# RWKV-7 in a two-layer trunk: the inverse applied inside the scan, with part of its work moved from TensorE to VectorE and from VectorE to GpSimd

## The chip, the cores and the metric

The kernel runs on one core of a Trainium2 chip, which has five engines with an instruction list of their own: TensorE (PE, matrix products into PSUM), VectorE (DVE), ScalarE (ACT), GpSimd (POOL) and SyncE (SP, which issues most of the DMA transfers). Each engine works through its list in order; semaphores make one wait for another. The metric is the device time of one execution in microseconds (us).

## What is computed

Two layers over 512 tokens of width 1024, in float32. Layer 0 has a Griffin recurrent block and RWKV-7 beside each other, layer 1 a gated DeltaNet and an mLSTM; each layer is followed by a squared-ReLU MLP. The change is in RWKV-7 (8 heads of 64), whose core is this, cut from the reference:

```
def step(S, inp):
    rt, wt, kt, vt, kkt, at = inp
    sk = jnp.einsum('bhvk,bhk->bhv', S, kkt)
    S = (S * wt[:, :, None, :] - sk[..., None] * (kkt * at)[:, :, None, :]
         + vt[..., None] * kt[:, :, None, :])
    return S, jnp.einsum('bhvk,bhk->bhv', S, rt)
...
y = jnp.concatenate([ya, yb], axis=-1) @ ev_w_out[e]
```

`ya` is the Griffin block's result, `yb` RWKV's after a norm over each head and a gate.

## The kernel before

The kernel takes RWKV's recurrence in 8 chunks of 64 tokens. Within a chunk the tokens' corrections depend on each other through a lower triangular 64x64 matrix for each head; the kernel inverts one plus that matrix, and with the inverse a chunk is a handful of 64x64 products, with the state `S` (64x64 for each head) handed from chunk to chunk. A product for all 8 heads of one chunk is 8 matmuls of 64x64. Most tiles hold two chunks; the inverse is made for two **halves** of four chunks each (`hf` 0 and 1, earlier and later tokens).

The class `Net` writes each engine's list at build time. The steps are generators ("streams"); a planner keeps a modelled clock for each engine and resumes the stream whose operands are ready, so the code's order isn't the list's order. All instructions go through one helper, so the profile gives them all line 73 and one goes by the tiles' names. These streams matter:

- The projections of the normed input (`ps_g<-hT,wh` and `ps_g<-hT,wl`: the weights' high and low parts, which VectorE, ScalarE and GpSimd make from `raw`, straight from memory). They come in the order of k, r, v, x (Griffin's input) and z (Griffin's gate).
- `product_stream` (from line 877) multiplies `va` (scaled kk and r) with `kb` (scaled k and kk·a), `ps_a<-va,kb` 64x128, and masks the results into `ab` (the matrix to be inverted), `bk` and `mm` (within a chunk). Before, its last quarter waits for the first half's inverse (`xb0`).
- `inverse_stream` (from 955), once for each half: it writes `ab` to memory (`d<-ab`) and reads it back as `q` so that each partition holds one 32x32 block. `lanes` (from 930) inverts the blocks by forward substitution, 31 steps of two operations (`xtmp<-xt,q`, then `xt<-xt,xtmp`), with between 16 and 136 elements in a partition. The result goes to memory (`d<-xt`) and comes back as `xb` with the blocks in their places (`xb<-d`, 8 transfers). To join two 32x32 blocks into a 64x64 inverse, TensorE transposes the blocks (`ps_a<-idn,xb`, 32 matmuls a half, copied to `xs`), multiplies them by `ab` (`xs,ab`, copied to `xg`) and by `xb` (`xb,xg`), and VectorE adds.
- `turn_stream` (from 902) transposes four tensors to token order (`ps_a<-idn,va` and `ps_a<-idn,kb`, copied to `tm`). Ahead of that `kb` is scaled by `pc` on GpSimd (`kb<-kb,pc`).
- `ahead_stream` (1014 to 1043) makes, for two chunks at a time, `wt` (`xb,tm`), `bv` (`tm,ab`) and `u0` (`bv,xb`).
- `scan_stream` (1045 to 1101) goes through the chunks: `u = u0 + wt·S` (`S,wt`, added by VectorE into `us`), the next state from `tm,tm` and `us,tm` (added to `tt`, the decayed state, which GpSimd makes from `S`), and the output from `tm,mm`, `S,va` and `us,mm`.
- `lru_stream` is the Griffin block: VectorE makes `xc` (the convolution) in three steps from PSUM, TensorE its gates (`xc,wlru`), GpSimd `i` and `r`, VectorE the scans (`th<-xc,i`), GpSimd `gel`, and VectorE the high and low parts `yah` and `yal`.
- `out_k` (709) is the Griffin half of the output projection (`wh,yah`, `wl,yah`, `wh,yal`; 96 matmuls in two column halves), which fills TensorE between the scan's steps; `out_y` is RWKV's half. `load_x` reads the residual `x` again.

Of the kernel before, what the change touches and what calls it, by code (L numbers as in the profile page):

```python
# [83 lines left out]
class Net:  # L84
# [792 lines left out]
    def product_stream(self):  # L877

        nc = self.nc
        self.ab, self.bk, self.mu, self.mv = [None] * 2, [None] * 2, [None] * 4, [None] * 4  # L880
# [3 lines left out]
        for m, hf in ((1, 0), (1, 1), (0, 0), (0, 1)):  # L884
            if m == 0 and hf:
                yield "xb0"
            ab, mm = (self.bk, self.mv) if m == 0 else (self.ab, self.mu)
            ab[hf] = self.slot(shape=(P, 4, 4, 64), tag="q", name="ab")
            for j in (2 * hf, 2 * hf + 1):
                mm[j] = self.slot(shape=(P, 2, 4, 64), name="mm")  # L890
            for c in range(4 * hf, 4 * hf + 4):
# [4 lines left out]
                for k, (o, mask) in enumerate(((ab[hf][:, c % 4], self.lt64), (mm[c // 2][:, c % 2], self.le64))):  # L896
# [5 lines left out]
    def turn_stream(self):  # L902

        nc = self.nc
        self.tm = [[None] * 4 for _ in range(4)]
        for p in range(4):
            yield f"v{p}"
        for hf in range(2):
            yield f"cm0{hf}"
            cs = slice(4 * hf, 4 * hf + 4)  # L910
# [4 lines left out]
            for k, src in ((1, self.va[:, 1]), (0, self.va[:, 0]), (2, self.kb[:, 0]), (3, self.kb[:, 1])):  # L915
# [14 lines left out]
    def lanes(self, d1, at):  # L930
# [25 lines left out]
    def inverse_stream(self, hf):  # L956
# [10 lines left out]
        lanes = self.lanes(d1.rearrange("g l s t -> (g l) s t"), at)  # L967
# [14 lines left out]
        for i in range(2):  # L982
            ps = yield from self.take()
            for l in range(8):
                for r in rows:
# [3 lines left out]
            self.give(ps)  # L989
# [1088 lines left out]
```

## Time and profile before

| | us |
|---|---|
| median of 3 runs (1371.24 to 1372.73) | 1372.07 |
| the profiled execution's own time | 1372.95 |
| its span in the trace | 1371.2 |

| engine | busy, us | share of the span |
|---|---|---|
| TensorE | 1309.5 | 95% |
| VectorE | 773.1 | 56% |
| ScalarE | 476.1 | 35% |
| GpSimd | 193.3 | 14% |

The busy share is an average over stages with different limits. A row of the timeline gives the start, the duration, the engine, the operation with its result and operands, the shape and the number of instructions merged, and in brackets the idle time of the engine before it and what released it. TensorE does each float32 matmul of 64x64 in two passes, so the trace has two records for one matmul of the list. TensorE's granted clock is 1.0 at full speed (2.4 GHz) and 0.5 at the lower level (1.2 GHz).

### The profile page before, as it was taken

The page shows a single profiled execution, that of the slowest core. Times are in us where ns is not written, and L with a number is a line of the kernel's source. Part 1 is how long each engine was busy: PE and PEld are TensorE (multiplying, and loading weights), DVE is VectorE, ACT ScalarE, POOL GpSimd, SP SyncE. Part 2 cuts the span into 40 slices and gives each one's busy share as a digit, 9 for nine tenths or more (in the row PEclk, how much of TensorE's full clock was granted, in tenths as well). Part 3 has the DMA queues.
Part 4 walks back from the last instruction along what each step waited for, and adds up shares of the span by engine and source line. Part 5 has one row for each costly group of instructions (what it writes and reads, how often), then busy time and mean ns, then how long its engine had stood idle before and what let it go on. Part 6 is the DMA issues. An engine that isn't in the chain of part 4 may idle for free.

```text
span 1371.2 us, 20609 instructions
## 1 busy us (share of the span) xinstructions
PE 1309.5 (95%) x8372; PEld 1078.5 (79%) x8372; DVE 773.1 (56%) x1435; ACT 476.1 (35%) x823; POOL 193.3 (14%) x172
## 2 busy tenths in 40 slices
PE   5899878999999999999999989999899999999998
PEld 5678668978888888888896777888688888888886
DVE  4896795466534445344567747854754354453544
ACT  5633452324322323223453434421343232232223
POOL 2362232131000000000013512212500000000000
PEclk9999998999999999999999999999999999999999
DMA  6123123032222222222312222110422222222221
GB/s 233 62 77 97 48 60 100 4 120 88 75 95 92 93 94 104 95 92 92 108 55 85 77 85 78 49 52 9 138 77 86 99 92 93 92 94 98 101 93 62
DMA packets 58453, 118.11 MB, mean 86 GB/s; under 512 B 17270, under 2 KB 17526, under 8 KB 58358
## 3 DMA queue, kind: packets, MB, share of 16 engines
q1 hardware_dynamic: 57062, 114.68, 24.8%
q10 hardware_dynamic: 1296, 2.11, 0.5%
q8 instruction: 66, 1.08, 0.3%
q14 instruction: 29, 0.24, 0.1%
HBM read 113.10 MB, written 3.67 MB: 85 GB/s over the span
## 4 chain that ended last, share of the span: by engine, by line
PE 81%; DVE 10%; ACT 3%; issue 2%; DMA 2%; POOL 1%; SPq 0%; DVEq 0%; POOLq 0%; ACTq 0%
PE ps_a L73 61%; PE ps_g L73 20%; DVE wl L73 1%; DMA q<-d1g 1%; DVE xn L73 1%; DVE xtmp L73 1%; DVE xt L73 1%; DVE th L73 1%; DVE sft L73 1%; DVE x L73 1%; DVE ktok L73 0%; DMA gb<-in_g_norm_dram 0%; POOL w L73 0%; ACT junk L73 0%; DVE cv L73 0%
## 5 line engine op out<-in xcount | busy, mean ns | idle before, releaser
L73 DVE TENSOR_TENSOR wl<-raw,wh 128x512 fp32r<-128x512 f32 x329 | 234.1, 717 | 255.9 <-ACT wh L73 246.4
L73 PE MATMUL ps_a<-hT,wh 128*128 128x512 f32 (+1 forms) x1088 | 312.5, 372 | 0.0
L73 ACT CAST wh<-raw 128x512 fp32r<-128x512 f32 x285 | 173.7, 619 | 367.7 <-PE ps_a L73 311.8
L73 PEld LDWEIGHTS ps_a<-hT,wh 128*128 128x128 f32 x1088 | 197.7, 188 | 36.5
L73 PE MATMUL ps_g<-hT,wh 128*128 128x512 f32 x656 | 217.5, 410 | 8.2 <-DVE xt L73 4.1
L73 PE MATMUL ps_a<-hT,wl 128*128 128x512 f32 (+1 forms) x544 | 202.9, 373 | 0.0
L73 PEld LDWEIGHTS ps_g<-hT,wh 128*128 128x128 f32 x656 | 125.4, 193 | 42.1 <-issue 13.6
L73 PE MATMUL ps_a<-wh,acth 128*128 128x512 f32 x384 | 151.6, 395 | 0.0
L73 PE MATMUL ps_a<-wh,actl 128*128 128x512 f32 x384 | 151.5, 394 | 0.0
L73 PE MATMUL ps_a<-wl,acth 128*128 128x512 f32 x384 | 151.4, 394 | 0.0
L73 PE MATMUL ps_g<-hT,wl 128*128 128x512 f32 x328 | 130.6, 398 | 0.0
L73 POOL TENSOR_TENSOR wl<-raw,wh 128x512 fp32r<-128x512 f32 x39 | 52.2, 1349 | 553.9 <-ACT wh L73 553.9
L73 PEld LDWEIGHTS ps_a<-hT,wl 128*128 128x128 f32 x544 | 102.3, 188 | 19.3
L73 PEld LDWEIGHTS ps_a<-wh,actl 128*128 128x128 f32 x384 | 72.2, 188 | 17.1
L73 DVE CAST wh<-raw 128x512 fp32r<-128x512 f32 x83 | 37.7, 454 | 84.9 <-PE ps_a L73 83.4
L73 PEld LDWEIGHTS ps_a<-wl,acth 128*128 128x128 f32 x384 | 72.1, 188 | 17.0
L73 PEld LDWEIGHTS ps_a<-wh,acth 128*128 128x128 f32 x384 | 72.1, 188 | 16.7
L73 ACT ACTIVATE relu<-ps_a 128x512 f32<-128x512 f32 x60 | 35.9, 599 | 138.7 <-PE ps_a L73 138.7
L73 PEld LDWEIGHTS ps_g<-hT,wl 128*128 128x128 f32 x328 | 63.1, 192 | 15.0 <-issue 1.4
L73 PE MATMUL ps_g<-hT,w 128*128 128x256 f32 x384 | 51.5, 291 | 0.5 <-DVE hT L73 0.5
L73 PE MATMUL ps_g<-wl,acth 128*128 128x512 f32 x128 | 50.5, 395 | 0.0
L73 PE MATMUL ps_g<-wh,actl 128*128 128x512 f32 x128 | 50.5, 394 | 0.0
(405 smaller groups left out, 1833.2 us busy)
## 6 DMA issues: line engine op xcount, KB each, us to landing
raw<-in_w_up_dram SPq DMA_DIRECT2D x64, 512.0 KB, 3.2
raw<-in_w_down_dram SPq DMA_DIRECT2D x64, 512.0 KB, 3.2
raw<-in_w_in_dram SPq DMA_DIRECT2D x47, 512.0 KB, 3.3
raw<-in_w_out_dram SPq DMA_DIRECT2D x32, 256.0 KB, 2.8
x<-in_x_dram SPq DMA_DIRECT2D x4, 512.0 KB, 9.3
x<-in_x_dram SPq DMA_DIRECT2D x8, 256.0 KB, 4.9
gb<-in_g_norm_dram ACTq DMA_DIRECT2D x8, 256.0 KB, 3.5
raw<-in_w_in1t_dram SPq DMA_DIRECT2D x8, 256.0 KB, 2.8
```

Of the source, the lines that this page charges most:

```text
L73: return fn(*args, **kw)
```

## The change

- The inverse is applied inside the scan. `ahead_stream` and its products are gone. For each chunk TensorE makes `bk·v`, adds `alpha·S` (`S,va`) in the same PSUM tile, the sum is copied to `us`, multiplied by `xb` (`us,xb`), and copied again as `u`. The transposes of alpha (half of `idn,va`) are gone with `wt`.
- Of the first products (`product_stream`) the last quarter no longer waits for the first half's inverse.
- The transposes of 32x32 blocks ahead of the join are 4 VectorE operations (128x512) instead of 64 matmuls and 4 copies.
- The substitution of the second half (`hf` 1) is on GpSimd, that of the first half and of layer 1 stays on VectorE.
- `turn_stream` does its second half when the scan is through chunk 1. `x` is read again in two parts, the second after the first column half of `out_k`.

The core of the diff:

```diff
@@ product_stream
-            if m == 0 and hf:
-                yield "xb0"
@@ turn_stream
+            if hf:
+                yield "go0"
...
-            for k, src in ((1, self.va[:, 1]), (0, self.va[:, 0]), (2, self.kb[:, 0]), (3, self.kb[:, 1])):
+            for k, src in ((0, self.va[:, 0]), (1, self.kb[:, 0]), (2, self.kb[:, 1])):
@@ lanes
-            nc.vector.tensor_tensor(out=tmp[:, :m, :n], in0=xt[:, :m, j:j + 1].broadcast_to([P, m, n]),
+            eng.tensor_tensor(out=tmp[:, :m, :n], in0=xt[:, :m, j:j + 1].broadcast_to([P, m, n]),
...
-            nc.vector.tensor_tensor(out=xt[:, :m, j + 1:32], in0=xt[:, :m, j + 1:32], in1=tmp[:, :m, :n], op=ALU.subtract)
+            eng.tensor_tensor(out=xt[:, :m, j + 1:32], in0=xt[:, :m, j + 1:32], in1=tmp[:, :m, :n], op=ALU.subtract)
@@ inverse_stream
-        lanes = self.lanes(d1.rearrange("g l s t -> (g l) s t"), at)
+        lanes = self.lanes(d1.rearrange("g l s t -> (g l) s t"), at, (nc.vector, nc.gpsimd)[hf])
...
-                    nc.tensor.matmul(ps[r, l * 64:l * 64 + 64], lhsT=xb[r, 8 * i + l, :], rhs=self.ident[r, r], start=True, stop=True)
...
-            self.cpy(xs[i].rearrange("p l t -> p (l t)"), ps)
+            nc.vector.transpose(out=xs[i].rearrange("p l t -> p (l t)"), in_=xb[:, 8 * i:8 * i + 8].rearrange("p l t -> p (l t)"))
@@ scan_stream (new; ahead(c) makes bk·v into w, k·v into s and mv·v into the output)
+            if c:
+                yield self.need(S0)
+                product(quarters(w), self.va[:, 1, :, c], S0, False, True)
+            bv = us[:, 0]
+            self.cpy(bv, quarters(w))
...
+            if c:
+                product(yv, self.va[:, 2, :, c], S0, False, False)
...
+            product(quarters(ps), self.xb[c // 4][:, c % 4], bv, True, True)
+            u = us[:, 1]
+            self.cpy(u, quarters(ps))
...
+                product(quarters(s), self.tm[2][j][:, h], u, False, True)
...
+            product(yv, self.mu[j][:, h], u, False, h == 1)
...
+            if c < 7:
+                w, s = yield from ahead(c + 1)
```

Over the whole program TensorE's list goes from 6822 to 6630 matmuls, VectorE's from 1437 to 1387 instructions, GpSimd's from 177 to 230. The next rows are the lists themselves, with no time in them.

GpSimd, from the clearing of the second half's `xt` on. `ab`'s mask is followed before by the two scalings of `kb`:

```order
47 L73 MEMSET xt_1015 64x16
48 L73 TENSOR_TENSOR ab_857<-ab_857,cst 128x1024 [waits DMAHW5_49,DMAHW6_49,DMAHW4_49,DMAHW7_49,DVE_49,Pool_49]
49 L73 TENSOR_TENSOR ab_904<-ab_904,cst 128x1024 [waits DMAHW2_49,DMAHW1_49,DMAHW3_49,DMAHW0_49,DVE_49]
50 L73 TENSOR_TENSOR kb<-kb,pc_104 128x4x256 [waits PE_49]
51 L73 TENSOR_TENSOR kb<-kb,pc_104 128x4x256
```

And in the changed kernel, at the same place:

```order
47 L73 MEMSET xt_1064 64x16
48 L73 TENSOR_TENSOR ab_857<-ab_857,cst 128x1024 [waits DMAHW5_49,DMAHW6_49,DMAHW4_49,DMAHW7_49,DVE_49,Pool_49]
49 L73 TENSOR_TENSOR ab_904<-ab_904,cst 128x1024 [waits DMAHW2_49,DMAHW1_49,DMAHW3_49,DMAHW0_49,DVE_49]
50 L73 TENSOR_TENSOR xtmp_1065<-xt_1064,q_1063 128x31 [waits DMAHW7_49]
51 L73 TENSOR_TENSOR xt_1064<-xt_1064,xtmp_1065 128x31 [waits Pool_49]
52 L73 TENSOR_TENSOR kb<-kb,pc_104 128x4x256 [waits PE_49]
53 L73 TENSOR_TENSOR xtmp_1065<-xt_1064,q_1063 128x30 [waits Pool_49]
54 L73 TENSOR_TENSOR xt_1064<-xt_1064,xtmp_1065 128x30 [waits Pool_49]
```

The first step of the second half's substitution, with its wait for `q`, now stands ahead of the one scaling of `kb` left there; the other is on VectorE.

SyncE, where the two halves' `q` are read (`q_923` is the first half's). Before:

```order
34 L73 DMA d_1_1009<-ab_904 32x16x32 [waits DMAHW3_49]
35 L73 DMA raw_1048<-in_w_in_dram 128x1024 [waits DMAHW4_49,DVE_49,Pool_49]
36 L73 DMA q_923<-d_0_907 128x1x1024 [waits DMAHW7_49,DMAHW6_49,DMAHW5_49]
37 L73 DMA raw_1092<-in_w_in_dram 128x1024 [waits DVE_49]
38 L73 DMA raw_1134<-in_w_in_dram 128x1024 [waits DVE_49]
39 L73 DMA q_1014<-d_1_1009 128x1x1024 [waits DMAHW2_49,DMAHW3_49,DMAHW1_49,DMAHW0_49]
```

And after:

```order
34 L73 DMA d_1_1058<-ab_904 32x16x32 [waits DMAHW3_49]
35 L73 DMA q_923<-d_0_907 128x1x1024 [waits DMAHW6_49,DMAHW7_49,DMAHW5_49,DMAHW4_49]
36 L73 DMA raw_1099<-in_w_in_dram 128x1024 [waits DVE_49,Pool_49]
37 L73 DMA raw_1141<-in_w_in_dram 128x1024 [waits DVE_49]
38 L73 DMA q_1063<-d_1_1058 128x1x1024 [waits DMAHW2_49,DMAHW3_49,DMAHW1_49,DMAHW0_49]
```

The first `q` moves ahead of a weight load, and the second stands behind two loads instead of three.

TensorE, between the last projection (z's fourth) and the first matmuls of `out_k` (`wh,yah`). Before (`ab_857` and `xb_1732` are the first half's):

```order
651 L73 MATMUL ps_g_1780<-hT_108,wl_1699 128x512
652 L73 MATMUL ps_a_1885<-idn,xb_1732 64x64 [waits DMAHW4_49,DMAHW3_49,DMAHW5_49,DMAHW2_49,Pool_49]
653 L73 MATMUL ps_a_1885<-idn,xb_1732 64x64 [waits DMAHW6_49,DMAHW7_49,DMAHW1_49,DMAHW0_49]
654 L73 MATMUL ps_a_1885<-idn,xb_1732 64x64 x14
655 L73 MATMUL ps_a_1904<-idn,xb_1732 64x64 x16
656 L73 MATMUL ps_g_1923<-wh_1746,yah_1849 128x512 [waits DVE_49,Activation_49]
```

And after (`xs_1895`, `xs_1897`, `ab_904` and `xb_1755` are the second half's):

```order
661 L73 MATMUL ps_g_1843<-hT_108,wl_1774 128x512
662 L73 MATMUL ps_a_1899<-xs_1895,ab_904 64x64 [waits DVE_49,Activation_49]
663 L73 MATMUL ps_a_1899<-xs_1895,ab_904 64x64 x15
664 L73 MATMUL ps_a_1918<-xs_1897,ab_904 64x64 [waits DVE_49,Activation_49]
665 L73 MATMUL ps_a_1918<-xs_1897,ab_904 64x64 x15
666 L73 MATMUL ps_a_1952<-xb_1755,xg_1916 64x64 [waits DMAHW2_49,DMAHW1_49,DMAHW3_49,DVE_49,DMAHW4_49,Activation_49,Pool_49]
667 L73 MATMUL ps_a_1952<-xb_1755,xg_1916 64x64 [waits DMAHW6_49,DMAHW7_49,DMAHW5_49,DMAHW0_49]
668 L73 MATMUL ps_a_1952<-xb_1755,xg_1916 64x64 x14
669 L73 MATMUL ps_a_1970<-xb_1755,xg_1935 64x64 [waits Activation_49]
670 L73 MATMUL ps_a_1970<-xb_1755,xg_1935 64x64 x15
671 L73 MATMUL ps_g_2002<-wh_1821,yah_1938 128x512 [waits DVE_49]
```

Where the first half's transposes stood, the whole join of the second half now stands ahead of `out_k`; the first half's join follows among `out_k`'s first matmuls. On VectorE the transposes for `xs` stand behind the last of the Griffin scans and ahead of the cast `yah`.

## Rows read from the trace of the kernel before

**Rows 1.** The page, parts 1 and 4: busy time, and the chain by engine.

```profile
PE 1309.5 (95%) x8372; PEld 1078.5 (79%) x8372; DVE 773.1 (56%) x1435; ACT 476.1 (35%) x823; POOL 193.3 (14%) x172
...
PE 81%; DVE 10%; ACT 3%; issue 2%; DMA 2%; POOL 1%; SPq 0%; DVEq 0%; POOLq 0%; ACTq 0%
```

**Rows 2.** Windows: start and end, length, each engine's busy time, clock, DMA share, GB/s.

```profile
158.00:198.00 40.00, 39.56 (x157) 29.56 (x156) 38.49 (x88) 23.52 (x32) 14.55 (x12) 0.98 0.14 47
198.00:213.00 15.00, 5.09 (x67) 4.14 (x67) 14.37 (x28) 7.15 (x12) 8.34 (x5) 0.71 0.66 196
213.00:300.00 87.00, 86.63 (x1977) 78.30 (x1978) 46.57 (x91) 27.08 (x48) 17.51 (x16) 0.97 0.15 45
```

**Rows 3.** Timeline of TensorE from 202 to 212 us, then of VectorE at 209 us.

```profile
202.28 0.44 PE L73 MATMUL ps_a<-idn,xb 64*64 64x64 f32 x2 [4.72 <-DMA xb<-d]
204.88 3.32 PE L73 MATMUL ps_a<-idn,xb 64*64 64x64 f32 x62 [2.17 <-DMA xb<-d]
211.27 0.77 PE L73 MATMUL ps_g<-wh,yah 128*128 128x512 f32 x1 [3.06 <-DVE yah L73]
...
209.71 1.42 DVE L73 CAST yah<-gel 128x512 fp32r<-128x512 f32 x1
```

**Rows 4.** Timeline of TensorE from 155 to 158 us.

```profile
155.74 3.00 PE L73 MATMUL ps_a<-xc,wlru 128*128 128x512 f32 x4 [3.97 <-issue]
157.75 1.42 PE L73 MATMUL ps_g<-hT,wh 128*128 128x512 f32 x1
```

**Rows 5.** Timeline of TensorE from 222 to 226 us: products.

```profile
222.78 1.92 PE L73 MATMUL ps_a<-va,kb 64*64 64x128 f32 x32
224.53 1.10 PE L73 MATMUL ps_a<-xb,tm 64*64 64x64 f32 x32
225.46 1.10 PE L73 MATMUL ps_a<-tm,ab 64*64 64x64 f32 x32
```

**Rows 6.** Timeline from 229 to 240 us: the state's copy and addition.

```profile
232.55 0.37 ACT L73 COPY S<-ps_a 128x256 f32<-128x256 f32 x1 [0.76 <-PE ps_a L73]
...
236.35 0.42 DVE L73 TENSOR_TENSOR S<-ps_a,tt 128x256 f32<-128x256 f32 x1 [1.44 <-PE ps_a L73]
```

**Rows 7.** Timelines: SyncE's issues of `q` and `xb`, then VectorE where `q` lands.

```profile
116.72 0.66 SPq L73 DMA_DIRECT2D q<-d  x1
...
128.00 0.54 SPq L73 DMA_DIRECT2D q<-d  x1
...
197.98 5.24 SPq L73 DMA_DIRECT2D xb<-d  x8
...
131.68 0.19 DVE L73 TENSOR_TENSOR xtmp<-xt,q 128x31 f32<-128x31 f32 x1 [1.49 <-DMA q<-d]
...
144.74 0.19 DVE L73 TENSOR_TENSOR xtmp<-xt,q 128x31 f32<-128x31 f32 x1 [8.03 <-DMA q<-d]
```

**Rows 8.** Groups of GpSimd by form: count, busy us, mean ns, idle before.

```profile
L73 POOL TENSOR_TENSOR wl<-raw,wh 128x512 fp32r<-128x512 f32 x39 | 52.2, 1349 | 553.9 <-ACT wh L73 553.9
...
L73 POOL TENSOR_TENSOR kb<-kb,pc 128x1024 f32<-128x1024 f32 x4 | 8.0, 2014 | 0.0
...
L73 POOL TENSOR_TENSOR tt<-S,pc 128x256 f32<-128x256 f32 x6 | 3.7, 620 | 54.0 <-DVE S L73 33.3 <-ACT S L73 20.7
...
L73 POOL COPY vx<-ei 128x4 f32<-128x4 f32 x4 | 0.9, 237 | 0.0
```

**Rows 9.** DMA issues by line: KB each, median us from issue to landing.

```profile
d<-xt SPq DMA_DIRECT2D x2, 256.0 KB, 4.1
```

**Rows 10.** Tile `xt`, both layers: count, minimum/median/maximum ns, first and last start.

```profile
L73 DVE TENSOR_TENSOR xtmp<-xt,q x93: 183/260/1415, 131.7 to 883.8; 128x126 f32<-128x126 f32 x9, 128x30 f32<-128x30 f32 x6, 128x56 f32<-128x56 f32 x6, 128x78 f32<-128x78 f32 x6
L73 DVE TENSOR_TENSOR xt<-xt,xtmp x93: 180/261/1390, 132.0 to 884.0; 128x126 f32<-128x126 f32 x9, 128x30 f32<-128x30 f32 x6, 128x56 f32<-128x56 f32 x6, 128x78 f32<-128x78 f32 x6
```

**Rows 11.** Timelines of GpSimd and VectorE from 169 to 172 us.

```profile
169.69 2.07 POOL L73 TENSOR_TENSOR r<-xc 128x512 f32<-128x512 f32 x2
...
170.78 1.12 DVE L73 TENSOR_TENSOR xt<-xt,xtmp 128x126 f32<-128x126 f32 x1
```

More of the change, by code (lines that the diff above doesn't have):

```diff
@@ L712, in out_k @@
             yield from self.acc_steps(acc, ys)
+            if load is not None and ch == 0:
+                load(x, 1)
             for t in range(NT):
@@ L904, in turn_stream @@
         nc = self.nc
-        self.tm = [[None] * 4 for _ in range(4)]
+        self.tm = [[None] * 4 for _ in range(3)]
         for p in range(4):
@@ L1048, in scan_stream, with product, ahead @@
         S = self.slot(shape=(P, 2, 4, 64), name="S")
+        us = self.slot(shape=(P, 2, 4, 64), name="us")
         self.in_parts(S, 256)
-        us = self.slot(shape=(P, 2, 4, 64), name="us")
         self.in_parts(us, 256)
-        quarters = lambda ap: ap.rearrange("p (q x) -> p q x", x=64)
+        quarters = lambda ap: ap[:, 0:256].rearrange("p (q x) -> p q x", x=64)
+        vy = {}
+        def product(out, a, b, start, stop):
+            for q, r in self.HEADS:
+                nc.tensor.matmul(out[r, q], lhsT=a[r, q], rhs=b[r, q], start=start and q == 0, stop=stop and q == 3)
+        def ahead(c):
+            j, h = c // 2, c % 2
+            yield f"tm2{j // 2}"
+            if h == 0:
+                psy = yield from self.take()
+                vy[j] = psy, psy.rearrange("p (c q x) -> p c q x", c=2, q=4)
+            v = self.tm[0][j][:, h]
+            w = yield from self.take()
+            product(quarters(w), self.bk[j][:, h], v, True, c == 0)
+            yield
+            s = None
+            if c < 7:
+                s = yield from self.take()
+                product(quarters(s), self.tm[1][j][:, h], v, True, False)
+                yield
+            product(vy[j][1][:, h], self.mv[j][:, h], v, h == 0, False)
+            return w, s
+        yield "cm00"
+        w, s = yield from ahead(0)
         for c in range(8):
@@ L1089, in scan_stream @@
+            yield f"xb{c // 4}"
+            yield self.need(bv, self.xb[c // 4])
+            ps = yield from self.take()
+            product(quarters(ps), self.xb[c // 4][:, c % 4], bv, True, True)
+            u = us[:, 1]
+            self.cpy(u, quarters(ps))
+            self.give(ps)
             yield self.need(u)
             if c < 7:
-                for q, r in self.HEADS:
-                    nc.tensor.matmul(v[r, q], lhsT=bt[r, h, q, :], rhs=u[r, q, :], start=False, stop=(q == 3))
+                product(quarters(s), self.tm[2][j][:, h], u, False, True)
@@ L1093, in scan_stream @@
                 if c:
-                    nc.vector.tensor_tensor(out=S1, in0=v, in1=tt, op=ALU.add)
+                    nc.vector.tensor_tensor(out=S1, in0=quarters(s), in1=tt, op=ALU.add)
                 else:
-                    self.cpy(S1, v)
-                self.give(ps)
-            for q, r in self.HEADS:
-                nc.tensor.matmul(vy[r, h, q], lhsT=mu[r, h, q, :], rhs=u[r, q, :], start=False, stop=(h == 1 and q == 3))
+                    self.cpy(S1, quarters(s))
+                self.give(s)
```

110 lines of the change are left out of this document (30 added, 80 removed).

## Prediction

> **What bounds the kernel now.** I read busy time and the chain first. TensorE is busy for 95% of the span and holds 81% of the chain that ended last [rows 1], so in most stretches an operation saved on TensorE is time saved and an edit elsewhere counts only where TensorE waits. The diff and the order of the instructions confine the change to layer 0, from RWKV's products (98 us) to the start of the second half of the output projection (about 300 us); behind that both kernels run nearly the same list. So I asked for windows of that stretch [rows 2]. From 213 to 300 us TensorE is busy for 86.63 of 87 us, while VectorE idles half the time: there TensorE's work is the price. From 198 to 213 us it is busy for 5.09 of 15 us at a granted clock of 0.71: it waits. From 158 to 198 us it is full, but VectorE is full too (38.49 of 40 us).
>
> Who releases it in the hole is the second reading. TensorE stops at about 197.6 us, waits 4.72 us and 2.17 us for the DMA that brings the first half's inverse back (`xb<-d`), runs 64 transposes slowly, and waits again until 211.27 us for VectorE's cast `yah` [rows 3]. I call 211.27 us, where the Griffin half of the output projection starts, the **gate**: what is saved on TensorE ahead of it is lost unless the gate moves too. `yah` is the end of VectorE's own chain: its row starts at 209.71 us, straight behind the last scan. Another hole ends at 155.74 us (3.97 us); the work behind it reads `xc`, which VectorE makes late between two sets of lane steps, and the first four matmuls then need 2.01 us, up to 157.75 us, and the next one 1.42 us: a slow restart, which I put at 2 us [rows 4].
>
> **Part 1, TensorE's work.** By the order 192 matmuls of 64x64 go (6822 to 6630). Sixteen of them are 32 records, and such a group takes 0.93 us (224.53 to 225.46), so 192 are 12 x 0.93 = 11.2 us [rows 5]. They don't go evenly. Ahead of the gate four product groups arrive that stood in the scan (4 x 0.875 = 3.5 us, from 222.78 to 224.53 for two), the second half's joining products (two groups more than the first half's transposes that stood there, 1.9 us) and chunk 0's first products (24 matmuls, 1.4 us), while two transposes of `va` go (1.9 us): +4.9 us. Behind the gate 11.2 + 4.9 = 16.1 us less remains. That stretch is full, so **-16.1 us** counts in full, if the gate stands where it stood.
>
> Three edits have one answer, nothing. The masks of the four earlier groups go with them to a time when VectorE's lanes haven't begun. The second half's transposes, held until chunk 1 is through, fill TensorE inside the scan instead of ahead of it. The reload of `x` in two parts is read only once the first half's projection is summed; if it came late, VectorE's additions would wait and, behind them, the buffers of the second half.
>
> **Part 2, the scan's chain.** Each chunk now runs S·va, copy, product with `xb`, copy, product with `tm`, add. By rows a product of 8 matmuls is half of 0.93 us, a copy 0.37 us on ScalarE and, like the add, about 0.42 us on VectorE [rows 5, 6]; with 0.1 us at each handover this is some 3 us a chunk, 24 us in all, against 66 us of TensorE work in the stretch. So it isn't the bound by sum; but TensorE's list is fixed, and behind each of the 16 copies it has only what stands there, mostly one or two other products, or two to four projection matmuls, against 0.6 us of copy and handover. VectorE's copies queue behind other work. Bounds: 0, and 0.5 us for each of 16 copies, 8 us. I take **+2.5 us**, nearer the lower end, since VectorE and ScalarE are half idle there [rows 2].
>
> **Part 3, the gate.** Three things must arrive; each is a sum.
>
> TensorE's own. The work that the gate's stretch starts with ends at 197.6 us before. To it come 3.5 + 1.4 - 1.9 = 3.0 us of moved work. The hole of 155.74 us should go, since VectorE has one set of lane steps there instead of two: -3.97 and -2.0 us (the other bound is 0). A new wait comes in. On GpSimd the first lane step now stands ahead of `kb<-kb,pc`, which TensorE's transposes `idn,kb` read. That step waits for `q`, the second half's matrices. `q` was issued at 128.00 us and used at 144.74 us, 16.7 us later; the first half's at 116.72 and 131.68, 15.0 us [rows 7]. In the new order SyncE issues the second one behind two weight loads instead of three, and by the wait for the second of these I place it near 125 us: landing 140 to 142 us, plus two small steps and 2.0 us for `kb` [rows 8] gives 142.5 to 144.5 us, where TensorE wants it near 140: +2.8 us (0.5 to 5), and VectorE's copy of `tm` waits behind it. Three weights' low halves (`wl`) also stand among GpSimd's lane steps: +1 us (0 to 4). Sum: 198.4 us.
>
> GpSimd's lanes. No lane step on GpSimd is in the trace, so I bound one. A multiply takes 620 ns for 256 and 2014 ns for 1024 elements, so 0.16 us + 1.82 ns an element; a copy of 4 elements takes 237 ns; `wl`, a subtraction, 1.349 us for 512, which is 1.25 times the multiply [rows 8]. One set's 31 multiplies have 2856 elements: 31 x 0.16 + 5.2 = 10.2 us, the subtractions 12.6 us, 23 us together, 29 us with 0.1 us at each dependence. Lower bound 23 us; upper bound 50 us, if VectorE gets in ahead of each (62 x 0.35 us more). From 143 us, with some 9 us between (three `wl`, two `i`, two `r` of 128x512, by `wl`'s row at most 9.4 us) and 7 us of interference, they end near 188 us (175 to 210). Writing out takes 4.1 us [rows 9], clearing and reading back `xb` about 8 us (the reads start at 197.98 us and release TensorE at 204.88 us now [rows 3, 7]): it is in place near 200 us.
>
> VectorE's chain. It loses 62 lane steps at a median of 0.26 us, 16 us [rows 10], and gets one `i` and one `r`, about 1.5 us by twice the addition of 256 elements [rows 6]. But the two engines shut each other out: VectorE's step `xt` from 170.78 us took 1.12 us while GpSimd's two `r` ran until 171.76 us [rows 11], and the slowest of the 93 steps `xtmp` took 1.415 us, five times the median [rows 10]. So GpSimd's 23 us of lane work can cost VectorE between 0 and 23 us; I take half, 12 us, since both have work that the other doesn't block. 209.7 - 16 + 1.5 + 12 = 207 us.
>
> The rule against this change is in the Trainium skill, SBUF — State Buffer, Who interferes with whom: a VectorE instruction with two SBUF inputs contends with a GpSimd instruction that reads SBUF, and the later one is blocked for the whole of the other. The step at 170.78 us, which ended just after GpSimd did, agrees. By the rule in full the 12 us would be 23 us; that is rival 1.
>
> So VectorE is last, at 207 us. Then two block transposes (no row has one; a copy of half this size takes 0.37 us, an addition 0.42 us [rows 6], so 1.5 us, up to 2.5 us), two product groups on a slow clock, two copies, two more groups: about 4.5 us. The gate comes near 213 us, **+2 us** (-5 to +13).
>
> The Trainium skill, VectorE: DVE Perf Modes, The three transpose paths, gives 311 ns for 128x128 in bf16; scaled by columns, an estimate from that page, one transpose here would be 1.2 us, and the gate 0.9 us later than I put it.
>
> **Sum.** -16.1 + 2.5 + 2 = -11.6 us on the profiled 1372.95 us: 1361.3 us. The median of the runs is 0.9 us lower, so I forecast **1360.5 us**. The clock around the gate stays as it is: TensorE idles ahead of it in both.
>
> **Rivals.**
> 1. The lock in full. VectorE pays 23 us, its scans end at 218 us, the gate at 224 us: 13 us late. -16.1 + 2.5 + 13 leaves about 1371 to 1372 us, within 0.2%. For it: the steps of [rows 10, 11]. Against it: VectorE's steps that read PSUM have no such row, and GpSimd's own fixed part need not hold it out. Chance 0.09.
> 2. Slower: GpSimd's steps. `xb` follows their end by 12 us and the gate that by 5 us, so the gain of 13.6 us is used up when they end at 208 us: (208 - 143 - 9) / 62 = 0.90 us a step instead of the 0.37 us of the rows (0.47 with handover). From there each 0.1 us costs 6.2 us; at 1.0 us a step, 1378 us. For it: nothing so small with two strided inputs is in the trace, and VectorE can hold it out. Against: the rows of 4 and 256 elements. Chance 0.11.
> 3. The scan waits: 8 us at the copies instead of 2.5 us gives 1366 us. For it: two copies a chunk in a fixed list. Against: half-idle copiers. Chance 0.15.
> 4. No mutual exclusion to speak of. VectorE is through at 196 us, TensorE and `xb` decide near 200 us, the gate is at 206 us: 1353.5 us. For it: VectorE loses 16 us where it is full [rows 2]. Against: [rows 11]. Chance 0.2.
>
> The forecast itself, 1356 to 1364 us, has 0.45. The range reaches from rival 4's lower side, 1352 us, to rival 1's upper end, 1372 us; what is left out is most of rival 2 and a little below. A measurement of this kernel can't tell less than 0.2% (2.7 us) from no change. Faster by more: 0.45 + 0.2 + 0.15 = 0.80; same: 0.09; slower: 0.11.
>
> **What would show it.** In the new profile TensorE should be busy for about 1298 us. The hole at 155 us should be gone and a wait for GpSimd's `kb` near 140 us should be there; if it's over 5 us, SyncE's order was misread. GpSimd's lane steps should sum to 23 to 35 us and end near 188 us; over 0.9 us each is rival 2. The first projection matmul on `yah` should start between 206 and 217 us; at 224 us it is rival 1. Idle of TensorE from there to the second half's start should be under 5 us; over 8 us is rival 3. The forecast is wrong if the gate leaves its range, or if TensorE's work behind the gate isn't near 66 us.

## The result, and the profile after

The changed kernel takes 1357.26 us (median) against 1371.65 us before: a ratio of 0.9891, 95% interval 0.9871 to 0.9910, so by the ratio 15 us less (12 to 18), by the medians 14 us. A single execution of 4492 us, of which there is no profile, is left out of the ratio; the median is over all four executions, that of the other three is 1357.05 us. The forecast was 1360.5 us with a range of 1352 to 1372 us, and faster. The profiled execution took 1355.24 us, its span is 1353.5 us.

The page after, parts 1 and 4 (as [rows 1]):

```profile
PE 1296.6 (96%) x7988; PEld 1065.2 (79%) x7988; DVE 768.0 (57%) x1385; ACT 467.5 (35%) x813; POOL 205.2 (15%) x225
PE 80%; DVE 10%; DMA 3%; ACT 3%; issue 2%; POOL 1%; SPq 1%; DVEq 0%; ACTq 0%; POOLq 0%
```

TensorE is busy for 12.9 us less (1298 us had been expected). Windows of the changed kernel, as [rows 2]:

```profile
158.00:198.00 40.00, 37.66 (x152) 28.03 (x150) 38.00 (x68) 24.51 (x35) 23.72 (x37) 1.00 0.22 63
198.00:213.00 15.00, 11.30 (x245) 10.30 (x247) 10.34 (x16) 7.67 (x13) 7.95 (x6) 0.89 0.49 151
213.00:300.00 87.00, 85.36 (x1457) 71.10 (x1454) 52.07 (x100) 24.97 (x54) 15.57 (x13) 1.00 0.22 75
```

The hole of 198 to 213 us, where TensorE worked for 5.09 us, now has 11.30 us of work, and its granted clock rose from 0.71 to 0.89. VectorE is still full ahead of it. The timeline of TensorE at the places that the prediction named, with the start of RWKV's half of the output projection (`ybh`) as the last row, and VectorE's last scan (as [rows 3, 4]):

```profile
140.81 3.95 PE L73 MATMUL ps_a<-idn,kb 64*64 64x64 f32 x128 [1.82 <-POOL kb L73]
...
201.14 3.47 PE L73 MATMUL ps_a<-xs,ab 64*64 64x64 f32 x64 [3.40 <-DVE xs L73]
...
206.56 0.50 PE L73 MATMUL ps_g<-wh,yah 128*128 128x512 f32 x1
...
281.41 0.39 PE L73 MATMUL ps_a<-wh,ybh 128*128 128x512 f32 x1
...
199.16 1.23 DVE L73 TENSOR_TENSOR_SCAN th<-xc,i 128x512 f32<-128x512 f32 x1
200.31 1.28 DVE L73 STREAM_TRANSPOSE xs<-xb 128x512 f32<-128x512 f32 x2
```

In the kernel before, the same start of RWKV's half is here:

```profile
301.18 0.40 PE L73 MATMUL ps_a<-wh,ybh 128*128 128x512 f32 x1
```

So 19.8 us are gained by the time RWKV's half starts; 1.2 us of them are there before the first product of the changed stretch (98.1 us before, 96.9 after), in code that is the same. Of the other 18.6 us, 3.5 us lie ahead of the gate (211.27 to 206.56 us) and 15.1 us behind it (89.9 to 74.85 us). Behind the start of RWKV's half both kernels do the same work, in 1070.0 us before and 1072.1 us after. This rest, with as many matmuls and no edit in it, took between 1067.6 us (e6) and 1076.0 us (e7) in the profiles below. It goes with the granted clock there: the three at 0.987 (e4, e5, e7) needed 1074 to 1076 us, the four at 0.992 and above (before, e2, e8, e12) 1070 to 1071 us. So a pair of profiles can't say more finely than several us what the medians hold.

GpSimd's list, as far as the steps (as [rows 7, 8]), then the steps as a tile with minimum, median and maximum ns, and SyncE's issue of the second `q`:

```profile
138.32 0.24 POOL L73 TENSOR_TENSOR xtmp<-xt,q 128x31 f32<-128x31 f32 x1 [25.53 <-DMA q<-d]
138.63 0.25 POOL L73 TENSOR_TENSOR xt<-xt,xtmp 128x31 f32<-128x31 f32 x1
138.84 1.92 POOL L73 TENSOR_TENSOR kb<-kb,pc 128x1024 f32<-128x1024 f32 x1
...
180.79 0.30 POOL L73 TENSOR_TENSOR xt<-xt,xtmp 128x16 f32<-128x16 f32 x1
...
L73 POOL TENSOR_TENSOR xtmp<-xt,q x31: 236/393/856, 138.3 to 180.2; 128x126 f32<-128x126 f32 x3, 128x30 f32<-128x30 f32 x2, 128x56 f32<-128x56 f32 x2, 128x78 f32<-128x78 f32 x2
L73 POOL TENSOR_TENSOR xt<-xt,xtmp x31: 238/411/880, 138.6 to 180.8; 128x126 f32<-128x126 f32 x3, 128x30 f32<-128x30 f32 x2, 128x56 f32<-128x56 f32 x2, 128x78 f32<-128x78 f32 x2
...
123.96 0.53 SPq L73 DMA_DIRECT2D q<-d  x1
```

The second `q` was issued at 123.96 us and landed 14.4 us later; the steps took 0.4 us each and ended at 181.1 us.

### The profile page after: what moved, and what is told of

Read it like the earlier page. It is cut to its first block, busy times and chain, and to the rows that moved or that the text cites. A ratio compares the mean times of both kernels' runs of the same rounds, so it can differ in the third digit from the quotient of the medians.

```text
span 1353.5 us, 19828 instructions
## 1 busy us (share of the span) xinstructions
PE 1296.6 (96%) x7988; PEld 1065.2 (79%) x7988; DVE 768.0 (57%) x1385; ACT 467.5 (35%) x813; POOL 205.2 (15%) x225
## 4 chain that ended last, share of the span: by engine, by line
PE 80%; DVE 10%; DMA 3%; ACT 3%; issue 2%; POOL 1%; SPq 1%; DVEq 0%; ACTq 0%; POOLq 0%
PE ps_a L73 60%; PE ps_g L73 20%; DVE wl L73 1%; DMA q<-d 1%; DMA q<-d1g 1%; DVE xn L73 1%; SPq L73 1%; DVE x L73 1%; DVE sft L73 1%; DVE xt L73 1%; DVE xtmp L73 1%; DMA gb<-in_g_norm_dram 1%; DVE ktok L73 1%; ACT junk L73 0%; DVE rs L73 0%
## 5 line engine op out<-in xcount | busy, mean ns | idle before, releaser
L73 PE MATMUL ps_a<-hT,wl 128*128 128x512 f32 (+1 forms) x544 | 202.7, 373 | 0.0
L73 POOL TENSOR_TENSOR wl<-raw,wh 128x512 fp32r<-128x512 f32 x35 | 47.4, 1360 | 516.4 <-ACT wh L73 516.4
L73 DVE CAST acth<-relu 128x512 fp32r<-128x512 f32 x64 | 27.4, 428 | 40.9 <-ACT relu L73 40.9
```

Source lines behind the costliest of these rows:

```text
L73: return fn(*args, **kw)
```

## The experiments

All numbers at a glance. "Gate" is the first matmul on `yah`, "RWKV's half" the first on `ybh`, both in us from the span's start of the profiled execution.

| kernel | median, us | ratio to before (interval) | gate | RWKV's half |
|---|---|---|---|---|
| before | 1371.65 | | 211.3 | 301.2 |
| changed | 1357.26 | 0.9891 (0.9871 to 0.9910) | 206.6 | 281.4 |
| a2 changed, again | 1356.95 | 0.9900 (0.9882 to 0.9918) | 207.5 | 281.7 |
| e1 steps on VectorE | 1367.33 | 0.9978 (0.9963 to 0.9993) | 206.0 | 288.5 |
| e2 transposes on TensorE | 1359.20 | 0.9926 (0.9904 to 0.9948) | 208.6 | 287.0 |
| e6 e1 and e2 together | 1365.92 | 0.9967 (0.9949 to 0.9985) | 208.6 | 296.5 |
| e4 kb ahead of the steps | 1358.32 | 0.9915 (0.9888 to 0.9941) | 209.2 | 286.8 |
| e8 joins late | 1356.85 | 0.9899 (0.9881 to 0.9918) | 202.8 | 284.8 |
| e7 GpSimd's steps doubled | 1370.74 | 0.9994 (0.9983 to 1.0005) | 216.8 | 293.3 |
| e5 all steps on GpSimd | 1368.31 | 0.9982 (0.9970 to 0.9994) | 202.7 | 293.6 |
| e10 before, q early | 1366.78 | 0.9975 (0.9960 to 0.9990) | 269.1 | 295.0 |
| e9 transposes early | 1361.85 | 0.9938 (0.9916 to 0.9959) | 205.5 | 286.4 |
| e11 changed, q early | 1351.83 | 0.9871 (0.9847 to 0.9895) | 251.7 | 276.0 |
| e12 e11 again | 1350.09 | 0.9857 (0.9836 to 0.9877) | 251.2 | 275.5 |

**e1: the steps of both halves on VectorE.**

```diff
-        lanes = self.lanes(d1.rearrange("g l s t -> (g l) s t"), at, (nc.vector, nc.gpsimd)[hf])
+        lanes = self.lanes(d1.rearrange("g l s t -> (g l) s t"), at, nc.vector)
```

> The changed kernel, but the substitution of both halves on VectorE. The changed kernel's fast runs are 1355.2 to 1357.5 us. Theory (GpSimd relieves VectorE, whose chain sets the gate): VectorE gets 62 steps of 0.25 us back, 15.7 us, and loses 8.4 us of interference on its own steps, so the Griffin scans end some 7 us later than at 200.3 us; TensorE's hole at 151 us, where it waits for xc, comes back with 3 to 5 us; the time is 1361 to 1366 us. Rival (the two engines shut each other out so far that GpSimd gives nothing): scans end at 199 to 202 us and the time is 1355 to 1358 us.

1367.33 us: 10 us of the 14 are gone, more than the theory's range, and the rival is out. But the picture is not the theory's. TensorE and VectorE in e1:

```profile
137.60 0.34 DVE L73 TENSOR_TENSOR xtmp<-xt,q 128x31 f32<-128x31 f32 x2 [4.55 <-DMA q<-d]
...
154.89 1.88 PE L73 MATMUL ps_a<-xc,wlru 128*128 128x512 f32 x4
...
206.04 0.77 PE L73 MATMUL ps_g<-wh,yah 128*128 128x512 f32 x1 [10.97 <-DVE yah L73]
```

The hole ahead of `xc,wlru` did not come back, although VectorE has both sets of steps: the row has no wait. And the gate is where the changed kernel has it. TensorE waits 10.97 us for it with nothing to do, since in e1's list both joins stand behind the gate. From the gate to RWKV's half e1 needs 82.5 us instead of 74.85 (64 matmuls more stand there, 3.7 us by [rows 5]), and from there to the first MLP activation 45.1 instead of 42.5 us.

**e2: transposes on TensorE again.**

```diff
-            nc.vector.transpose(out=xs[i].rearrange("p l t -> p (l t)"), in_=xb[:, 8 * i:8 * i + 8].rearrange("p l t -> p (l t)"))
+            ps = yield from self.take()
+            for l in range(8):
+                for r in rows:
+                    nc.tensor.matmul(ps[r, l * 64:l * 64 + 64], lhsT=xb[r, 8 * i + l, :], rhs=self.ident[r, r], start=True, stop=True)
+            self.cpy(xs[i].rearrange("p l t -> p (l t)"), ps)
+            self.give(ps)
```

> The changed kernel, but the blocks transposed on TensorE again with copies to xs. Theory: 64 matmuls come back, 3.7 us; half of them stand ahead of the gate, where TensorE waits 3.4 us anyway, so 1.9 us counts and a copy more in the chain of the join; VectorE is rid of 2.6 us: 1357 to 1360 us. Rival (the transposes on VectorE hold the gate up, since VectorE is full until then): 1354 to 1356 us.

1359.20 us, as the theory had it: 2 us for 64 matmuls. The interval of its ratio touches both of the changed kernel's, so these 2 us are at the edge of what can be told.

**e6: both of these, so that the new scan stands alone.**

> The changed scan with both other parts undone: substitution of both halves on VectorE and block transposes on TensorE. Theory: TensorE's work behind the gate is still some 14 us less than before, but the gate stands where it stood (211 us) or 2 us later: 1360 to 1367 us. Rival (the scan carries all the gain): 1355 to 1358 us.

1365.92 us: the scan alone keeps 4 to 5 of the 14 us. In steps from there: steps on GpSimd give 6.7 us (to e2), transposes on VectorE on top of them 2 us (to the changed kernel); transposes on VectorE without GpSimd give nothing (e1 is 1.4 us above e6, within what the two intervals allow). The parts need each other. TensorE behind e6's gate, a window from the gate to RWKV's half, and the waits in it:

```profile
208.50:296.50 88.00, 82.98 (x1712) 70.99 (x1713) 47.81 (x88) 22.96 (x46) 18.25 (x15) 0.96 0.24 71
...
PE ps_a L73 <- DVE yn L73: 2.4, 2, 1.3
PE ps_g L73 <- DVE x L73: 1.7, 1, 1.7
```

TensorE is idle for 5 us there. The waits shown, 4.1 us of them, are for the norm `yn` and for the residual's additions to `x`; no wait over 0.15 us is for the scan's new copies (`us`). The clock stays at 0.96.

**e4: nothing ahead of the scaling of `kb` on GpSimd.** The lanes of the second half wait for a flag that `turn_stream` sets behind its first two scalings.

```diff
         yield next(lanes)
+        if hf:
+            yield "kbs0"
...
                 self.tt(w, w, self.pc[:, :, cs, None].broadcast_to([P, 4, 4, 64]), ALU.mult)
+            self.set(f"kbs{hf}")
```

> The changed kernel, but the second half's first step on GpSimd waits until kb has been scaled for the first half, so that nothing stands ahead of that scaling. Theory (the gate is VectorE's, and TensorE waits 3.4 us for it): the wait of 1.82 us at 140.8 us goes, the gate moves by less than 1 us, the time is 1355.5 to 1357.5 us, not told from the changed kernel. Rival (each wait of TensorE counts in full): 1.8 us less, 1353.5 to 1355.5 us.

1358.32 us: the new wait is gone, and nothing is gained; not told from the changed kernel, as the theory said, though the time lies just above the theory's range and the gate came 2.6 us later in its profile, not under 1 us. In that profile (its slowest execution) the 1.82 us came back further on, as a wait of 4.07 us for `xc`, where the changed kernel has 1.52 us:

```profile
173.03 1.19 PE L73 MATMUL ps_g<-hT,wh 128*128 128x512 f32 x2 [4.07 <-DVE xc L73]
```

**a2: the changed kernel again**, beside the next three.

> The changed kernel itself, beside the next three on the same chip: 1355 to 1359 us. Its TensorE waits before the first projection matmul on yah should again sum to 2.5 to 5 us.

1356.95 us; the wait for `xs` is 3.4 us again.

**e8: the joins behind the gate.** GpSimd keeps its steps; `inverse_stream` waits for a flag that layer 0 sets as it begins `out_k`.

```diff
         rows = [slice(0, 64), slice(64, P)]
+        yield "gate"
         yield self.need(xb, A)
...
         yield self.need(*self.ya[3])
+        self.set("gate")
         yield from self.out_k(self.ya, x, self.load_x)
```

> The changed kernel, but the joins of both halves wait until the Griffin half of the output projection is begun, as they stood with the lanes on VectorE alone; the lanes stay where they are. Theory 2 (GpSimd's steps pay because the second half's inverse is ready while TensorE waits for VectorE, so that its join of 3.7 us fills that hole and keeps the clock up): the hole grows to 6 to 9 us, the gate comes at 203 to 206 us, the start of the second half of the output projection is 4 to 7 us later than in the changed kernel, the time 1361 to 1364 us. Rival (GpSimd's steps pay because VectorE is rid of its own): 1355 to 1358.5 us.

1356.85 us: no slower, so theory 2, which I had formed from e1, falls. The gate, with the join off its way:

```profile
202.78 0.77 PE L73 MATMUL ps_g<-wh,yah 128*128 128x512 f32 x1 [4.86 <-DVE yah L73]
```

It is 3.8 us earlier than in the changed kernel, and RWKV's half 3.4 us later. Beside e1, whose order is the same at this place, the steps on GpSimd bring the gate from 206.0 to 202.8 us, and TensorE waits 4.86 us there instead of 10.97 us. What GpSimd gives is VectorE's time after all; whether it's taken as an earlier gate (e8) or as a join done ahead of it (the changed kernel) makes no difference that can be measured. By the profiles e8 is 6 us ahead of e1 at the first MLP activation (327.3 and 333.6 us); the whole profiles 9.1 us and the medians 10.5 us apart. So some 3 us of the other 4 arise behind that activation, where both do the same work, at a granted clock of 0.994 in e8 and 0.989 in e1; why the clock differs stays open.

**e7: GpSimd's steps made longer.** Each multiplication is issued three times.

```diff
+            if eng is nc.gpsimd:
+                for _ in range(2):
+                    eng.tensor_tensor(out=tmp[:, :m, :n], in0=xt[:, :m, j:j + 1].broadcast_to([P, m, n]),
+                                      in1=at[:, j:j + 1, j + 1:32].broadcast_to([P, m, n]), op=ALU.mult)
```

> The changed kernel, with each multiplication of GpSimd's steps issued three times, so that a step pair costs about twice: GpSimd ends near 208 to 212 us instead of 181 us, at about 0.9 us for each operation of the original count. Rival 2 of the prediction (the gate follows GpSimd's end by 17 us): the gate near 225 us and the time 1368 to 1376 us. Theory: the order puts the first half's join, which is VectorE's, into the hole instead, and the second half's inverse is needed only for chunk 4, near 240 us; only the longer interference counts, 2 to 5 us on VectorE: 1358 to 1363 us.

1370.74 us, a ratio of 0.9994: the whole gain is gone. The steps are busy for 60.5 us instead of 26.2 us, 2.3 times as long, and end at 222.2 us, later than I had reckoned. Rival 2's time is met, but not by its way: the gate follows not the second half's inverse but GpSimd's list. Timelines of e7 on GpSimd, ScalarE and TensorE:

```profile
210.67 1.26 POOL L73 TENSOR_TENSOR gel<-gel,th 128x512 f32<-128x512 f32 x1
...
211.96 0.62 ACT L73 CAST yah<-gel 128x512 fp32r<-128x512 f32 x1 [9.18 <-POOL gel L73]
...
213.99 0.58 ACT L73 COPY xg<-ps_a 128x512 f32<-128x512 f32 x1
...
214.67 2.17 PE L73 MATMUL ps_a<-xb,xg 64*64 64x64 f32 x32 [5.58 <-POOL xtmp L73]
216.77 0.79 PE L73 MATMUL ps_g<-wh,yah 128*128 128x512 f32 x1
```

`gel` stands in GpSimd's list behind most of the longer steps; ScalarE's list stands still for 9.18 us at the cast that needs it, with the join's copy `xg` behind; TensorE gets `xg` at 214.67 us. (The row names `xtmp`, GpSimd's last event then; the copy is what it multiplies.) By rival 2's sum, a gate 17 us behind the last step, it would have been at 239 us.

**e5: all steps on GpSimd.**

```diff
-        lanes = self.lanes(d1.rearrange("g l s t -> (g l) s t"), at, (nc.vector, nc.gpsimd)[hf])
+        lanes = self.lanes(d1.rearrange("g l s t -> (g l) s t"), at, nc.gpsimd)
```

> The changed kernel with both halves' substitution on GpSimd. Theory 2: VectorE is rid of 24 us, its scans end before TensorE's projections (198 us), but 124 steps of 0.47 us and 13 us of other work keep GpSimd until some 200 us and the joins to 212 us, behind the gate, while the scan has to wait for them: gate 199 to 203 us, 1357 to 1364 us. Rival (VectorE's relief is what pays): 1350 to 1355 us.

1368.31 us, beyond the ranges of theory 2 and of its rival. The gate is early (202.7 us), VectorE has time, and it doesn't help: GpSimd's steps last until 206 us. TensorE's waits between 98 and 300 us in e5 (sum, count, longest):

```profile
PE ps_a L73 <- DVE xs L73: 6.7, 1, 6.7
PE ps_g L73 <- DVE yah L73: 5.4, 1, 5.4
PE ps_g L73 <- DVE yal L73: 3.2, 1, 3.2
```

**e10: the kernel before, with `q` asked for earlier.** It moves SyncE's two reads of `q` to where the changed kernel has them.

```diff
-        yield self.need(d1)
+        yield self.need(d1) - 4
         nc.sync.dma_start(out=at.rearrange("l s t -> l (s t)"), in_=d1.rearrange("l s t -> l (s t)")[None].broadcast_to([2, 64, 1024]))
```

> The kernel before (its scan, its lanes on VectorE), with one change: both halves' q are asked for up to 4 us earlier in the planner's time, so that SyncE's list has the first q ahead of a weight load and the second behind two loads, as in the changed kernel. This also moves other work: the Griffin half of the projection comes behind the scan. Question: why TensorE's hole of 3.97 us at 155.74 us is gone in the changed kernel. Theory (VectorE's list stands still for 8 us behind the second half's first step, which waits for q, so xc is late): the hole goes with the early q although both sets of steps stay on VectorE, and VectorE's wait shrinks to 2 to 6 us. Rival (two sets of steps on VectorE make xc late): the hole stays at 3 us or more. The time is expected within 1365 to 1385 us and decides nothing.

The theory holds. VectorE, and the work that had waited ([rows 4, 7]):

```profile
138.73 0.34 DVE L73 TENSOR_TENSOR xtmp<-xt,q 128x31 f32<-128x31 f32 x2 [2.30 <-DMA q<-d]
...
152.26 1.88 PE L73 MATMUL ps_a<-xc,wlru 128*128 128x512 f32 x4
```

VectorE's wait of 8.03 us shrinks to 2.30 us, and TensorE's hole of 3.97 us is gone with both sets of steps on VectorE. Much else moved in this kernel (its gate is at 269.1 us), so its time says nothing of the hole; but e1, where it hadn't, shows no hole either.

**e9: the block transposes earlier.** `yield self.need(xb, A) - 3` in place of `yield self.need(xb, A)`, ahead of them.

> The changed kernel, with VectorE's block transposes 3 us earlier in the planner's time, so that they stand ahead of the last two Griffin scans instead of behind them. Theory (the join waits for the transposes, and the gate for the join): TensorE's hole at 198 us shrinks from 3.4 us to under 1.5 us, the gate comes at 204.5 to 206 us, the time is 0 to 2 us less: 1355 to 1357 us. Rival (xb is not there that early, so VectorE waits with the scans behind it): the gate at 207 to 210 us, 1358 to 1361 us.

1361.85 us: both times missed, though the gate is where the theory had it. The wait for `xs` at the hole is gone and the gate is 1 us earlier, but the planner made other choices behind it: the casts of `yah` went to ScalarE, and the first half's join came later. Timeline of TensorE in e9, then a window behind its gate:

```profile
205.47 0.50 PE L73 MATMUL ps_g<-wh,yah 128*128 128x512 f32 x1 [2.62 <-ACT yah L73]
207.45 0.79 PE L73 MATMUL ps_g<-wh,yal 128*128 128x512 f32 x1 [1.15 <-DVE yal L73]
212.36 1.97 PE L73 MATMUL ps_a<-xs,ab 64*64 64x64 f32 x32 [1.55 <-DVE xs L73]
...
206.00:215.00 9.00, 6.30 (x42) 4.61 (x42) 6.40 (x6) 2.96 (x5) 5.48 (x4) 0.50 0.42 139
```

TensorE now waits between the join and the gate, and behind it the granted clock is at its lower level, 0.50, where the changed kernel has 1.00. From the gate to RWKV's half e9 needs 80.9 us instead of 74.85: work at half the clock makes some 3 to 4 us of the difference (an estimate, half of the 6.30 us in this window and a little behind it), and 2 us are more waiting.

**e11: the changed kernel with `q` early**, as e10 but with 8 in place of 4.

> The changed kernel with both halves' q asked for up to 8 us earlier in the planner's time: the second half's q stands behind one weight load, both scalings of kb ahead of GpSimd's first step, and the planner lets the scan run among the last projections, with the Griffin half of the output projection behind it. Theory (the hole ahead of the gate can be filled by the scan): no wait for yah, no wait for kb, 1348 to 1355 us. Rival (the inverse comes later on the chip than in the planner's time, since a q takes 14 to 16 us to land, so TensorE's list stands behind it): a wait of 5 us or more ahead of the first xs product, 1358 to 1370 us.

1351.83 us, better than both kernels. With the inverse due earlier, the planner lets the scan run among the last projections, and the Griffin half of the output projection follows it. On the chip the transfer itself comes little earlier: GpSimd's first step starts at 136.73 us instead of 138.32 us. Windows of e11, then that step:

```profile
138.00:198.00 60.00, 59.23 (x767) 47.03 (x763) 49.91 (x90) 31.67 (x46) 42.09 (x72) 1.00 0.22 63
198.00:213.00 15.00, 14.71 (x440) 13.96 (x438) 11.81 (x23) 5.24 (x10) 1.64 (x3) 1.00 0.02 4
213.00:300.00 87.00, 82.17 (x953) 66.77 (x949) 56.63 (x99) 30.80 (x63) 16.77 (x13) 1.00 0.30 98
...
136.73 0.37 POOL L73 TENSOR_TENSOR xtmp<-xt,q 128x31 f32<-128x31 f32 x1 [7.90 <-DMA q<-d]
```

The hole is full: 14.71 us of 15 at full clock. There is no gate any more; `yah` is ready when TensorE comes to it but for 1.9 us. So what pays here is the new order; the earlier transfer and the order were not tried apart.

**e12: the same again**, over more executions.

> The kernel of the last experiment again (the changed kernel with both q asked for early), timed over more rounds. If its gain over the changed kernel is real: 1350 to 1354 us, a ratio to the kernel before of 0.985 to 0.989. If the first result was a lucky set of runs: 1355 to 1358 us and 0.989 to 0.991, as the changed kernel.

1350.09 us, a ratio of 0.9857 (0.9836 to 0.9877), clear of the changed kernel's second 0.9900 (0.9882 to 0.9918); the first, 0.9891 (0.9871 to 0.9910), still touches it.

## Why the prediction was right, point by point

The sign, the size and the place came out, with three terms mis-sized or misread that partly made up for each other. Part of it is luck: the profiled execution, 1355.24 us, lies 6.1 us under the 1361.3 us of the sum, mostly by the gate, and the median lies nearer only because the medians gain 14 us where the profiles gain 18.

**TensorE's work behind the gate** was put at -16.1 us plus 2.5 us of waits; measured 15.1 us less. The two windows, from the gate to RWKV's half, before and after:

```profile
211.20:301.20 90.00, 89.16 (x1985) 79.90 (x1986) 49.56 (x93) 28.08 (x50) 19.77 (x18) 0.96 0.17 53
...
206.50:281.40 74.90, 73.14 (x1493) 61.97 (x1489) 43.51 (x85) 20.23 (x41) 14.25 (x12) 1.00 0.21 69
```

Busy time falls by 16.0 us, as summed, and idle time rises by 0.9 us (0.84 to 1.76), at the low end of the 0 to 8 us for the scan's copies. Neither of the two waits that make it up is for a copy of the scan (0.56 us for the first half's `xs`, 1.20 us for the norm `yn`). So the scan isn't bound by its chain. But "the clock around the gate stays as it is" was wrong: the join now stands straight ahead of the gate, and the stretch runs at a granted 1.00 instead of 0.96, which gives some 3.6 us. Where TensorE waits at the gate instead, 10.97 us in e1, 4.86 us in e8 and 2.62 us in e9, the first 4 to 9 us behind it have 0.50. The 3.6 us are lost again at a term that I hadn't: between the two kinds of work. The timeline of TensorE in the changed kernel:

```profile
244.52 0.39 PE L73 MATMUL ps_a<-wh,yah 128*128 128x512 f32 x1
244.84 0.68 PE L73 MATMUL ps_a<-us,xb 64*64 64x64 f32 x16
245.45 0.50 PE L73 MATMUL ps_a<-wl,yah 128*128 128x512 f32 x1
245.79 0.40 PE L73 MATMUL ps_a<-wh,yal 128*128 128x512 f32 x1
246.02 0.39 PE L73 MATMUL ps_a<-wh,yah 128*128 128x512 f32 x1
```

A projection matmul takes 0.23 us from start to start (245.79 to 246.02) but 0.32 and 0.34 us beside a product, and the product 0.61 instead of 0.47 us: 0.34 us for one interlude. Such changes of form number 24 before and 42 after in this stretch; 18 more at 0.17 us are 3.1 us. That this is what eats the clock's gain is a sum that fits, not an experiment. The prediction's sign for this stretch, work of TensorE near 66 us, was missed as it stands: the window has 73.14 us of it, and 89.16 - 16.1 would have been 73.1 us. The same matmuls at the spacing that they have within one form (0.93 us for 32 records, 0.23 us for a projection matmul) come to some 65 us, an estimate; so the 66 us seem to have left out the changes of form.

**The gate** was put 2 us later; it came 4.7 us earlier (3.5 us, with the common start taken off), at the very edge of the 206 to 217 us stated for it. Of its three arrivals:
- TensorE's own end of the projections was put at 198.4 us; it waits from 197.7 us. The wait for `kb` exists, 1.82 us against 2.8 us. By e4's time it was worth nothing.
- GpSimd's steps: 26.2 us of work against 23 to 35 us expected; their end 181.1 us instead of 188 us, since they began at 138.3 us instead of 143 us and took 42.8 us from first to last instead of 45 us.
- VectorE's last scan ends at 200.4 us, not 207 us. This is the arrival that set the gate. The last scan before, then in e1, which differs from the changed kernel in the second half's steps alone:

```profile
207.61 2.17 DVE L73 TENSOR_TENSOR_SCAN th<-xc,i 128x512 f32<-128x512 f32 x1
...
203.33 1.22 DVE L73 TENSOR_TENSOR_SCAN th<-xc,i 128x512 f32<-128x512 f32 x1
```

It ends at 204.6 us in e1, so moving the second set of steps gave 4.2 us, as between e6 and e2 (207.1 and 202.9 us); my terms for that (-16, +1.5, +12) come to 2.5 us. The other 5.2 us are there with both sets on VectorE, and the sum doesn't have them at all. 1.5 us of them are e1's earlier start (first product at 96.6 us); for the rest the rows show VectorE's wait for the second `q`, 8.03 us before, 4.55 us in e1 and 2.30 us in e10, where the scans of the kernel before end at 202.1 us. So the term that failed is one left out, this wait; and the two large terms were both too large and made up for each other. The steps' own busy time (windows with tile `xtmp`; VectorE, then GpSimd), before, after, and in e1:

```profile
131.00:204.00 73.00, 33.95 (x124) 0.96 0.17 56
...
129.60:188.00 58.40, 23.94 (x62) 26.23 (x62) 1.00 0.19 62
...
129.30:203.40 74.10, 31.80 (x124) 0.98 0.21 66
```

The relief is 33.95 - 23.94 = 10.0 us, 7.9 us beside e1, and not 16 us: two sets of steps overlap in part (their durations add up to 39.3 us before). The exclusion can be read step by step, each against the lower quartile of the steps of its shape in five profiles (before, changed, a2, e1, e8). A step with nothing beside it on GpSimd takes its usual time in all of them. In the changed kernel 28 of the 62 steps run beside GpSimd's steps and take 3.4 us longer together, and 15 beside its larger operations take 5.2 us longer, 8.6 us in all. But VectorE's chain before was already paying for GpSimd's large operations, of which [rows 11] shows one: 45 of its 124 steps took 8.5 us longer. So 12 us were charged for next to nothing that was new. The same goes for the last two scans: 1.22 and 2.17 us before, the second under GpSimd's `gel`; 1.22 and 1.23 us after, since `gel` begins only at 200.4 us. The rule from the Trainium skill, SBUF — State Buffer, Who interferes with whom, is borne out as a mechanism, by these steps. Charged in full, as rival 1 did, it would have put the scans at 218 us; they were at 200.4 us.
- The chain from there to the gate took 6.2 us (200.3 to 206.56 us), as put (6 us). The two transposes took 1.28 us together (1.5 us put). The estimate scaled by columns from the Trainium skill, VectorE: DVE Perf Modes, The three transpose paths, had given 2.4 us for the two; the measurement decides.

**The hole at 155.74 us** went, as forecast with 6 us, but the reason given was wrong. It was not that VectorE had one set of steps less: e1 has both sets and no hole. It was that VectorE's list stood still for 8.03 us at the second half's first step, which waited for a `q` that SyncE had issued behind three weight loads; e10 shows it in the kernel before. I had both rows, [rows 4] and [rows 7], and didn't put them together.

**Rival 2**, slower by GpSimd's steps, is bounded by e7: with the steps 2.3 times as long nothing of the gain is left. Its threshold (0.90 us a step, 2.1 times the 0.42 us measured) was about right, its mechanism wrong: in e7 the gate followed what stands among the steps on GpSimd (`gel`), not the second half's inverse. **Rival 3** did not happen (0.9 us more idle instead of 8 us). **Rival 4**, 1353.5 us, came near for the gate's part (206 us). Its reason, no exclusion to speak of, is half right: there is exclusion, but hardly more than before; VectorE was through at 200.4 us, not 196 us.

What stays open: the profile of the changed kernel gains 18.6 us where the kernels differ and the medians 14 us; the rest of the program gives 2 to 3 us back in both profiles of the changed kernel (1072.1 and 1073.3 us against 1070.0 us), within the 1067.6 to 1076.0 us of kernels that don't differ there.

## What to carry to other kernels

Price an edit at the point where the engines next meet: what TensorE saves ahead of that point is worth nothing, and what it saves behind it is worth its time, here 16.0 us of busy time for the 16.1 us summed, with a gain at the clock and a cost of changes of form that cancelled. When work moves to an engine that shares its way to memory, look first whether the engine it leaves already pays for that sharing (8.5 us before, 8.6 us after), and then what stands behind the moved work in the new engine's list, since that, more than the moved work's own end, sets the delay (e7). And follow a hole back through every list to its transfer: a wait that one engine shows for another's result was here a DMA that stood behind three weight loads. Asking for it earlier removed the hole in the kernel before (e10). In the changed kernel it gave the best time of all (e12, 1350.1 us), but through the order that the planner then wrote, since the transfer itself moved by only 1.6 us.

## What the runs showed of the hardware that I had not expected

- GpSimd's small operations are cheap for their size: 0.24 us for 30 or 31 elements in a partition and some 0.43 us for 126 to 136, with two inputs, against 0.19 and 0.29 us on VectorE (medians, in the changed kernel and the kernel before).
- VectorE's transpose of 32x32 blocks, 128x512 in float32, takes 0.66 to 0.70 us, and two in a row 1.28 us; a copy of that size out of PSUM takes 0.69 us.
- On TensorE a short run of 64x64 products between matmuls of 128x512 costs some 0.34 us beside its work, by the rows at 244.52 to 246.02 us above.
- A `q` of 512 KB, which repeats 64 rows of 4 KB for two halves of the partitions, lands 14.4 us after its issue, where a weight load of that size lands in 3.2 to 3.3 us. Two windows of the changed kernel show where the time goes: with only `q` under way 0.13 of the 16 DMA engines are busy, which is two of them; with a weight load beside it 0.90.

```profile
127.00:130.50 3.50, 3.50 (x15) 2.53 (x15) 1.83 (x5) 1.20 (x2) 0.00 (x0) 1.00 0.13 51
131.50:133.00 1.50, 1.50 (x9) 1.22 (x8) 1.12 (x4) 0.91 (x2) 0.00 (x0) 1.00 0.90 270
```

Why `q` gets only two is not shown. Its source is given as two copies of 64 rows, and no run tried another shape, which might be worth more than asking earlier.
